# Block sums made in the raw weight buffer, one buffer layout for the whole MLP, and more loads issued by GpSimd, in a one-core hybrid decoder layer

## The chip, the cores and the metric

The kernel runs on one core of a Trainium2 chip. The metric is the device time of one execution in microseconds (us), as a median over runs. The trace belongs to one profiled execution of the same program. In the text TensorE is the engine of matrix products (PE in the profile, with its weight loads shown as PEld), VectorE is DVE, ScalarE is ACT, GpSimd is POOL, and SyncE is SP, which here only issues DMAs. Each engine takes its instructions in the order in which they were put down for it.

## The reference, cut to what matters

One decoder layer with D = 2048, 512 tokens, an MLP width of 8192, all in float32:

```python
mod = silu(c) @ w_ada + b_ada            # six vectors: sh1, sc1, gt1, sh2, sc2, gt2
h = rmsnorm(x) * (1 + sc1) + sh1
q, k, v, xr, xg = split(h @ w_in)        # 3 x 1024 attention, 2 x 1024 recurrence
mixed = concat(rmsnorm(stick_breaking(q, k, v)), rmsnorm(rg_lru(conv(xr)) * gelu(xg)))
x = x + gt1 * (mixed @ w_out)
h = rmsnorm(x) * (1 + sc2) + sh2
hid = square(relu(h @ w_mlp_in))         # 2048 x 8192
x = x + gt2 * (hid @ w_mlp_out)          # 8192 x 2048
return rmsnorm(x, g_norm_final)
```

The change concerns the lines from `mixed @ w_out` to `hid @ w_mlp_out`.

## The kernel before, in words

**Data.** Features lie on the 128 partitions and the 512 tokens in the columns, so a 128x512 tile is one block of 128 features. Every float32 operand of a product is split in two: a high half, which ScalarE makes by a copy into a narrower format, and a low half, which VectorE makes by subtracting the high half from the original (`low`, L115; every low half of the kernel has this line). A product is then three matmuls: high by high, high by low, low by high (`mm3`, and L944 to L946 in the MLP).

**Ordinary products.** `weights` (L193) loads a 128x512 block of weights into `wr` (or `raw` where there is no `wr`), splits it into `wh` and `wl` (ScalarE L207, VectorE L115), and the matmuls of L222 to L226 use it. The output product `mixed @ w_out` is done in four groups of 512 output features. Groups 0 to 2 run on all 512 tokens. Group 3, the last, is done in two token halves A and B of 256 (L872 to L880), so that the norm of half A can begin while half B is multiplied. `out_evac` (L729) then makes x1 = x + gt1 * y, with a scaled addition per tile (L737) and a square and sum for the norm (`add_square`, L299; the sum is L304). Group 0 of `w_mlp_in` is also done by ordinary products in two halves (L885 and L891); at L889 the buffer regions are switched. In all, the last output product and this group are four half products of 16 weight blocks each. The text calls the stretch in which they run the entry to the MLP.

**Block products.** The other 15 groups of `w_mlp_in` and all of `w_mlp_out` use a Strassen-like scheme: a 2x2 arrangement of blocks multiplied by seven products instead of eight. `operands` (L898) loads one block of four quarters (128 x 4 x 256 floats, 512 KB) into `raw` and prepares seven operands: three of the quarters as they are, and four sums of quarters. Per block the instructions are: a sum of 512 columns (L905) and two of 256 (L912, L913), all into a separate tile `ts`; the high copy of three raw quarters by ScalarE (L911, 128x768) and their low half by VectorE (L115, 128x768), both into `w3` tiles; the high copy of the four sums by ScalarE (L917, 128x1024) and their low half by VectorE (L115, 128x1024), both into `w4` tiles. TensorE uses a block in 42 matmuls of 256 columns. `strassen` (L928) runs such blocks, eight to a group in the first phase, into seven PSUM banks, and `combine` (L956) recombines the banks with one ScalarE copy and seven VectorE steps (L960 to L966).

**First MLP phase** (`w_mlp_in`, L1010). After each group `keep_parts` (L827) squares the four results, splits them, forms four sums (L847), and writes all to DRAM as `part` and `sum` through GpSimd's queue. One group is eight blocks.

**Second MLP phase** (`w_mlp_out`, L1084). There are 124 blocks in runs of up to eight for one of four output groups n = 0 to 3. Unfinished banks are written to DRAM as `prod` (GpSimd, L1126) and later loaded back (`load_pre`, L1069, SP) as seed `pre` tiles, which ScalarE copies into PSUM (L934). `load_pair` (L980) brings `part` and `sum` tiles back through SP, and `later_split` splits the sums (ScalarE L994, VectorE L115). Beside it `ada_late` (L1025) makes the last modulation vector: 64 loads of 128x512 into `st` through SP, with one VectorE step each (L1040).

**What sets the order.** The program is written as one sequence; a list scheduler lays it out for each engine by priority. `tc.high_priority` moves a piece forward (URGENT for weights, SETW for `operands`, SETE for evacuations). Side work (norms, `sums`, `keep_parts`, `ada_late`) comes from generators in three lanes, of which `tick` after each weight block takes a few steps. Buffers are pools with a fixed number per name: a new use of a name waits for the old use of the buffer to end. A stage (`STAGES`) is a region of the on-chip memory with its own names; going from one to the next, the new tiles wait for the old ones in that place. Before, there are three: "front", "mlp_in" (`raw` 3, `ts` 2, `w4` 6, `w3` 6) and "mlp_out" (`raw` 3, `ts` 2, `w4` 4, `w3` 4, `pre` 7, `st` 2). `sums` (L806) makes the sums of the activations for the seven products.

The functions that the change touches:

## Time and profile before

| | |
|---|---|
| median of 3 runs | 2160.44 us |
| runs | 2158.01, 2160.44, 2169.7 us |
| profiled execution, whole | 2159.86 us |
| profiled execution, span of the trace | 2158.2 us |
| granted TensorE clock, mean | 0.984 of full speed |
| until 706 us | projections, attention, recurrence, output groups 0 to 2 |
| 706 to 835 us | the entry: last output product, group 0 of `w_mlp_in`, first block products |
| 868 to 1387 us | 13 groups of the first phase |
| 1428 to 1470 us | the turn from the first to the second phase |
| 1512 to 2052 us | most of the second phase |

The profile has a page (busy time of each engine, the span in slices, DMA queues, the chain that ended last, the costliest groups of instructions, DMA issues) and the trace can be asked for parts. In a row of a group of instructions there stand the line, the engine, the operation, output and input tiles, shape and count, then the busy time with the mean of one in ns, then the idle time of the engine just before these instructions with what ended it. `<-ACT w L911` means that the wait ended when ScalarE had written a `w` tile in line 911. All `w3`, `w4` tiles are named `w` there. In rows of a timeline the first number is the start, the second the duration, both in us. In rows of waits, such as `a <- b: 11.0, 2, 10.7`, there stand the time in all, how many, and the longest.

### The profile page before, as it was taken

Reading aid. Unit: us, or ns where it says so; the run is one execution under the profiler, and the core shown is the slowest. Engines: PE = TensorE matmul, PEld = TensorE weight load, DVE = VectorE, ACT = ScalarE, POOL = GpSimd, SP = SyncE. Lnnn points to the kernel's source line nnn. Section 1 sums busy time; section 2 is a strip of 40 time slices with the busy share of each in tenths; the row PEclk is TensorE's granted clock in tenths of the full one; section 3 lists DMA queues with packets and bytes.
Section 4 is the critical chain, followed back from the end, with each engine's and each line's share of the span. In section 5 each row is a group of like instructions: output and inputs, shape, how many; then the busy total and the mean of one; then the engine's idle time right before and its main releaser. Section 6 shows DMA issues by size and latency. Waiting matters only on the chain.

```text
span 2158.2 us, 38620 instructions
## 1 busy us (share of the span) xinstructions
PE 2042.1 (95%) x14532; PEld 1907.9 (88%) x14532; DVE 1800.3 (83%) x3026; ACT 1107.8 (51%) x1657; POOL 180.2 (8%) x276
## 2 busy tenths in 40 slices
...
GB/s 287 281 292 239 202 146 139 164 146 181 234 254 317 252 143 179 165 199 167 150 202 157 167 186 165 191 324 304 259 217 316 304 232 287 254 274 260 309 144 113
DMA packets 225053, 475.06 MB, mean 220 GB/s; under 512 B 22497, under 2 KB 45153, under 8 KB 224866
## 3 DMA queue, kind: packets, MB, share of 16 engines
...
q14 instruction: 73, 0.60, 0.1%
...
## 4 chain that ended last, share of the span: by engine, by line
PE 35%; issue 26%; DMA 16%; DVE 13%; POOL 5%; ACT 3%; SPq 1%; POOLq 0%; DVEq 0%; ACTq 0%
DMA x<-in_w_adaT_dram 5%; PE ps_mm L222 3%; PE ps_mm L226 3%; PE ps_mm L225 3%; DVE w L115 3%; DMA raw<-in_w_mlp_out_dram 3%; POOL part L839 3%; PE ps_mm L946 3%; PE ps_mm L944 2%; PE ps_mm L945 2%; DMA st<-in_w_adaT_dram 2%; POOL sum L848 2%; DMA a<-sum 2%; PE ps_z L946 2%; PE ps_z L944 2%
## 5 line engine op out<-in xcount | busy, mean ns | idle before, releaser
L946 PE MATMUL ps_mm<-a,w 128*128 128x256 f32 x1704 | 483.4, 285 | 10.4 <-DVE w L115 9.9
L944 PE MATMUL ps_mm<-a,w 128*128 128x256 f32 x1704 | 482.9, 284 | 5.5 <-ACT w L911 5.3
L945 PE MATMUL ps_mm<-a,w 128*128 128x256 f32 x1704 | 481.2, 283 | 0.0
L911 ACT ACTIVATE w<-raw 128x768 fp32r<-128x768 f32 x244 | 205.5, 842 | 435.1 <-issue 124.9
L944 PE MATMUL ps_z<-a,w 128*128 128x256 f32 x1288 | 366.1, 284 | 19.9 <-ACT w L911 12.8
L946 PE MATMUL ps_z<-a,w 128*128 128x256 f32 x1288 | 366.5, 285 | 6.2 <-DVE w L115 6.2
L945 PE MATMUL ps_z<-a,w 128*128 128x256 f32 x1288 | 364.3, 283 | 0.0
L946 PEld LDWEIGHTS ps_mm<-a,w 128*128 128x128 f32 x1704 | 322.7, 190 | 15.4 <-DVE w L115 15.0
L944 PEld LDWEIGHTS ps_mm<-a,w 128*128 128x128 f32 x1704 | 324.0, 190 | 7.1 <-ACT w L911 6.1
L945 PEld LDWEIGHTS ps_mm<-a,w 128*128 128x128 f32 x1704 | 323.8, 190 | 0.0
L115 DVE TENSOR_TENSOR w<-raw,w 128x768 fp32r<-128x768 f32 (+1 forms) x262 | 244.5, 934 | 71.0 <-ACT w L911 67.0
L115 DVE TENSOR_TENSOR w<-ts,w 128x1024 fp32r<-128x1024 f32 x244 | 297.6, 1220 | 3.3 <-ACT w L917 3.1
L917 ACT ACTIVATE w<-ts 128x1024 fp32r<-128x1024 f32 x244 | 255.8, 1049 | 42.4 <-DVE ts L913 37.8
L944 PEld LDWEIGHTS ps_z<-a,w 128*128 128x128 f32 x1288 | 244.6, 190 | 22.3 <-ACT w L911 14.0
L946 PEld LDWEIGHTS ps_z<-a,w 128*128 128x128 f32 x1288 | 244.4, 190 | 9.6 <-DVE w L115 9.2
L181 DVE SCALAR_TENSOR_TENSOR x<-x,cb 128x1024 f32<-128x1024 f32 x160 | 195.5, 1227 | 64.0 <-DMA x<-in_w_adaT_dram 63.4
L945 PEld LDWEIGHTS ps_z<-a,w 128*128 128x128 f32 x1288 | 244.7, 190 | 0.0
L207 ACT ACTIVATE wh<-wr 128x512 fp32r<-128x512 f32 x232 | 142.9, 619 | 194.5 <-PE ps_mm L225 90.7
L905 DVE TENSOR_TENSOR ts<-raw 128x512 f32<-128x512 f32 x244 | 167.3, 687 | 69.7 <-DMA raw<-in_w_mlp_out_dram 59.5
L222 PE MATMUL ps_mm<-a,wh 128*128 128x512 f32 (+1 forms) x528 | 201.0, 381 | 8.7 <-DVE a L401 3.1
L226 PE MATMUL ps_mm<-a,wl 128*128 128x512 f32 (+1 forms) x528 | 200.0, 380 | 2.7 <-DVE wl L115 2.6
L115 DVE TENSOR_TENSOR wl<-wr,wh 128x512 fp32r<-128x512 f32 x232 | 158.5, 686 | 50.1 <-ACT wh L207 49.4
...
## 6 DMA issues: line engine op xcount, KB each, us to landing
x<-in_w_adaT_dram SPq DMA_DIRECT2D x160, 512.0 KB, 5.2
raw<-in_w_mlp_out_dram SPq DMA_DIRECT2D x124, 512.0 KB, 4.7
...
wr<-in_w_in_dram SPq DMA_DIRECT2D x160, 256.0 KB, 3.7
...
```

The lines of the kernel that those rows point to most:

```text
L115: tt(out=out, in0=full, in1=f32(high), op=ALU.subtract)
L181: stt(out=t, in0=t, scalar=1.0, in1=cb[q * n // 1024][:, o : o + n], op0=ALU.mult, op1=ALU.mult, accum_out=ga[:, q : q + 1],)
L207: act(h[:, :n], r[:, :n], AF.Copy)
L222: first = mm(out, wh, ah, start=start, stop=False, **kw)
L225: mm(out, wh, al, start=False, stop=False, **kw)
L226: mm(out, wl, ah, start=False, stop=stop, **kw)
L905: tt(out=t[:, : 2 * HT].rearrange("p (a b) -> p a b", a=2), in0=r[:, HT : 3 * HT].rearrange("p (a b) -> p a b", a=2), in1=r[:, q_(0)].unsq ...
L911: act(h, r[:, HT:], AF.Copy)
L917: act(h, t, AF.Copy)
L944: mm(out, wh[:, blk(i)], ah, start=st, stop=False, **kw)
L945: mm(out, wh[:, blk(i)], al, start=False, stop=False, **kw)
L946: mm(out, wl[:, blk(i)], ah, start=False, stop=j == js[-1], **kw)
```

## The change

It has four parts.

1. *Block sums in the raw buffer.* `operands` makes the four sums as four additions of 256 columns in place, in `raw`, one after another (new L924), after the high copy and the low half of the raw quarters have read it. `ts` is gone; the 128x1024 copy and low half now read `raw`. So the old order per block was sums, copy and low half of quarters, copy and low half of sums, and the new order is copy and low half of quarters, sums, copy and low half of sums.
2. *One layout.* The regions "mlp_in" and "mlp_out" become one, "mlp" (`raw` 3, `w4` 6, `w3` 6, `nb` 2), opened ahead of the last output product; the second switch is gone. `n` (5 tiles) becomes permanent. The last output product and group 0 load through `raw` (three buffers, where `wr` had four) and split into `w4`. Seeds use `n` and `nb`, late modulation uses `a`, and the sums of activations two `nb`.
3. *Half products.* A new `half_product` puts four results of 256 columns into two PSUM banks, where four banks were used half. The sums of activations and half operands are made when they are asked for.
4. *Loads and writes by GpSimd.* The 16 writes of x1, the 98 loads of seeds (`pre`) and the 64 loads of late modulation are issued by GpSimd instead of SP.

The core of the diff:

```diff
+BUFS = {"cb": 2, "a": 64, "ga": 4, "n": 5}
 STAGES = {
-    "front": {"x": 3, "tt": 5, "wr": 4, "wh": 3, "wl": 3, "n": 5},
-    "mlp_in": {"raw": 3, "ts": 2, "w4": 6, "w3": 6},
-    "mlp_out": {"raw": 3, "ts": 2, "w4": 4, "w3": 4, "pre": 7, "st": 2},
+    "front": {"x": 3, "tt": 5, "wr": 4, "wh": 3, "wl": 3},
+    "mlp": {"raw": 3, "w4": 6, "w3": 6, "nb": 2},
 }
...
 def operands(src):
             r = T("raw")
             nc.sync.dma_start(r.rearrange("p (c f) -> p c f", c=2), src)
-            t = T("ts")
-            tt(
-                out=t[:, : 2 * HT].rearrange("p (a b) -> p a b", a=2),
-                in0=r[:, HT : 3 * HT].rearrange("p (a b) -> p a b", a=2),
-                in1=r[:, q_(0)].unsqueeze(1).broadcast_to([P, 2, HT]), op=ALU.add,
-            )
             h, lo = T("w3", F32R), T("w3", F32R)
             act(h, r[:, HT:], AF.Copy)
-            tt(out=t[:, q_(2)], in0=t[:, q_(0)], in1=r[:, q_(2)], op=ALU.add)
-            tt(out=t[:, q_(3)], in0=t[:, q_(2)], in1=r[:, q_(3)], op=ALU.add)
             low(lo, r[:, HT:], h)
+            for i, j in ((1, 0), (0, 2), (2, 1), (3, 2)):
+                tt(out=r[:, q_(i)], in0=r[:, q_(i)], in1=r[:, q_(j)], op=ALU.add)
             h, lo = T("w4", F32R), T("w4", F32R)
-            act(h, t, AF.Copy)
-            low(lo, t, h)
+            act(h, r, AF.Copy)
+            low(lo, r, h)
...
+    def half_product(bs, src, operand, ks):
+        for k in ks:
+            wh, wl = weights(src(k), "w4")
+            ah, al = operand(k)
+            for o, out in enumerate(halves(bs)):
+                mm3(
+                    out, wh[:, blk(o)], wl[:, blk(o)], ah, al, k == ks[0] and o % 2 == 0, k == ks[-1],
+                    skip_group_check=True,
+                )
+            tick()
...
+    stage("mlp")
     r2 = T("n")
     order = A_ + L_
-    product(ba, out_src(3), mx, order, A)
+    half_product(b2, out_src(3), mixed_half(A), order)
...
-    for k in range(NK):
-        nc.sync.dma_start(x1D[k], x1[k])
+    for k in range(12, NK):
+        nc.gpsimd.dma_start(x1D[k], x1[k])
...
-    stage("mlp_out")
...
-            t = T("st")
-            tc.keep_in_program_order(nc.sync.dma_start(t, w_adaT[...]))
+            t = T("a")
+            tc.keep_in_program_order(nc.gpsimd.dma_start(t, w_adaT[...]))
...
     def load_pre(n):
-        ts = [T("pre") for _ in range(7)]
+        ts = [T("n" if i < 5 else "nb") for i in range(7)]
         for t, d in zip(ts, prodD[n]):
-            nc.sync.dma_start(t, d)
+            nc.gpsimd.dma_start(t, d)
```

The scheduler lays the instructions out anew. The first place is VectorE at the start of the last output product. The rows are line, operation, output and inputs, shape; `wl` or, after, the second `w4` is the low half of a block of `w_out`; `a` in line 737 (734 after) is an x1 tile of output group 2, and L304 (L301 after) adds its square to the sum for the norm. Before:

```order
L115 TENSOR_TENSOR wl_1345_6573<-wr_1343_6570,wh_1344_6572 128x512
L115 TENSOR_TENSOR wl_1348_6591<-wr_1346_6588,wh_1347_6590 128x512
L737 SCALAR_TENSOR_TENSOR a_1330_6475<-ps_mm_1269_6159,mods_69,n_1331_6476 128x512
L737 SCALAR_TENSOR_TENSOR a_1332_6481<-ps_mm_1270_6160,mods_69,n_1333_6482 128x512
L737 SCALAR_TENSOR_TENSOR a_1334_6487<-ps_mm_1271_6161,mods_69,n_1335_6488 128x512
L115 TENSOR_TENSOR wl_1351_6609<-wr_1349_6606,wh_1350_6608 128x512
L304 TENSOR_TENSOR n_1060_5282<-n_1060_5282,n_1331_6476 128x512
L737 SCALAR_TENSOR_TENSOR a_1336_6493<-ps_mm_1272_6162,mods_69,n_1337_6494 128x512
L115 TENSOR_TENSOR wl_1354_6627<-wr_1352_6624,wh_1353_6626 128x512
```

The same place after:

```order
L734 SCALAR_TENSOR_TENSOR a_1329_6474<-ps_mm_1268_6158,mods_69,n_1330_6475 128x512
L734 SCALAR_TENSOR_TENSOR a_1331_6480<-ps_mm_1269_6159,mods_69,n_1332_6481 128x512
L734 SCALAR_TENSOR_TENSOR a_1333_6486<-ps_mm_1270_6160,mods_69,n_1334_6487 128x512
L301 TENSOR_TENSOR n_1059_5281<-n_1059_5281,n_1330_6475 128x512
L734 SCALAR_TENSOR_TENSOR a_1335_6492<-ps_mm_1271_6161,mods_69,n_1336_6493 128x512
L301 TENSOR_TENSOR n_1059_5281<-n_1059_5281,n_1332_6481 128x512
L301 TENSOR_TENSOR n_1059_5281<-n_1059_5281,n_1334_6487 128x512
L301 TENSOR_TENSOR n_1059_5281<-n_1059_5281,n_1336_6493 128x512
L112 TENSOR_TENSOR w4_1345_6577<-raw_1344_6575,w4_1345_6577 128x512
```

The first low halves of the last output product stood ahead of and between the scaled additions of group 2; now all four scaled additions and all four sums stand ahead of the first low half.

The second place is VectorE in the first MLP phase, blocks near the end of a group, where no recombination step stands between them. The first two rows of a block are the two low halves (of the quarters, 128x768, and of the sums, 128x1024), the others its sums. Before:

```order
L115 TENSOR_TENSOR w3_2265_12530<-raw_2262_12525,w3_2264_12529 128x768
L115 TENSOR_TENSOR w4_2267_12536<-ts_2263_12527,w4_2266_12535 128x1024
L905 TENSOR_TENSOR ts_2286_12660<-raw_2285_12658 128x512
L912 TENSOR_TENSOR ts_2286_12660<-ts_2286_12660,raw_2285_12658 128x256
L913 TENSOR_TENSOR ts_2286_12660<-ts_2286_12660,raw_2285_12658 128x256
L115 TENSOR_TENSOR w3_2271_12588<-raw_2268_12583,w3_2270_12587 128x768
L115 TENSOR_TENSOR w4_2273_12594<-ts_2269_12585,w4_2272_12593 128x1024
L905 TENSOR_TENSOR ts_2296_12732<-raw_2295_12730 128x512
```

After:

```order
L924 TENSOR_TENSOR raw_2379_14484<-raw_2379_14484 128x256 x4
L112 TENSOR_TENSOR w4_2383_14495<-raw_2379_14484,w4_2382_14494 128x1024
L112 TENSOR_TENSOR w3_2386_14545<-raw_2384_14542,w3_2385_14544 128x768
L924 TENSOR_TENSOR raw_2384_14542<-raw_2384_14542 128x256 x4
L112 TENSOR_TENSOR w4_2388_14553<-raw_2384_14542,w4_2387_14552 128x1024
L112 TENSOR_TENSOR w3_2402_14620<-raw_2400_14617,w3_2401_14619 128x768
L924 TENSOR_TENSOR raw_2400_14617<-raw_2400_14617 128x256 x4
L112 TENSOR_TENSOR w4_2404_14628<-raw_2400_14617,w4_2403_14627 128x1024
L112 TENSOR_TENSOR w3_2411_14692<-raw_2409_14689,w3_2410_14691 128x768
```

Before, the sums of a later block (`ts_2286`) stood between the low halves of an earlier one and the next, and a block's sums came two low-half pairs ahead of its own low halves. After, a block is finished from its first low half to its last before the next is begun.

99 lines of the change are left out of this document (51 added, 48 removed).

## The prediction

> **What bounds the kernel now.** I began with the page's first part, to see which engine the span follows.
>
> ```profile
> span 2158.2 us, 38620 instructions
> PE 2042.1 (95%) x14532; PEld 1907.9 (88%) x14532; DVE 1800.3 (83%) x3026; ACT 1107.8 (51%) x1657; POOL 180.2 (8%) x276
> ```
>
> TensorE (PE) is busy 95% and VectorE (DVE) 83%: an average over stages, so I cut the span by stage, with the view of busy time by stretch. The columns are: length, then PE, PEld, DVE, ACT and POOL busy with instruction counts, then granted clock, DMA share, GB/s.
>
> ```profile
> 706.00:823.00 117.00, 97.93 (x772) 94.52 (x771) 96.29 (x198) 78.89 (x160) 0.00 (x0) 0.96 0.62 194
> 786.00:798.00 12.00, 1.36 (x5) 1.07 (x5) 10.39 (x26) 11.72 (x29) 0.00 (x0) 0.69 0.00 0
> 823.00:835.00 12.00, 7.37 (x35) 6.02 (x35) 10.48 (x19) 8.18 (x15) 0.66 (x1) 0.72 0.32 102
> 868.00:1387.00 519.00, 519.00 (x4376) 519.00 (x4375) 470.10 (x704) 267.03 (x364) 89.75 (x130) 1.00 0.55 172
> 1428.00:1470.00 42.00, 27.17 (x175) 25.72 (x174) 37.83 (x63) 21.65 (x33) 12.75 (x20) 0.76 0.81 283
> 1512.00:2052.00 540.00, 515.12 (x4187) 504.87 (x4187) 440.51 (x734) 272.37 (x374) 43.60 (x81) 0.99 0.77 271
> ```
>
> The fourth row is the first MLP phase. There TensorE never stops: 519 us for 4376 matmuls of 256 columns, 0.1186 us each. I use that pace as TensorE's own speed and count matmuls elsewhere. A weight block of the MLP takes 42 matmuls, so 4.98 us.
>
> Entry to the MLP (706 to 835, rows 1 and 3): 807 matmuls, 95.7 us of TensorE, took 129 us, so 33 us are lost. Row 2 is the largest hole: no DMA, half clock. Turn from the first to the second phase (row 5): 175 matmuls are 20.8 us, so 21 of 42 us are lost. Second phase (row 6): 4187 matmuls are 497 us, so 43 of 540 us are lost, at 5.42 us a block. These three stretches, some 97 us, are what the change can win. In row 4 it can only lose. VectorE there is busy 470 of 519 us, so I looked at its spare time next.
>
> ```profile
> L115 DVE TENSOR_TENSOR w<-raw,w 128x768 fp32r<-128x768 f32 x104 | 99.1, 953 | 41.9 <-ACT w L911 41.9
> L917 ACT ACTIVATE w<-ts 128x1024 fp32r<-128x1024 f32 x104 | 108.6, 1044 | 0.1
> L847 DVE TENSOR_TENSOR a<-a,a 128x512 f32<-128x512 f32 x52 | 35.5, 682 | 2.9 <-DMA part<-a 2.1 <-DMA sum<-a 0.6
> L115 DVE TENSOR_TENSOR a<-a,a 128x512 fp32r<-128x512 f32 x39 | 26.6, 683 | 0.0
> 868.65 0.68 DVE L960 TENSOR_TENSOR a<-ps_z,a 128x512 f32<-128x512 f32 x1
> 1386.98 0.68 DVE L960 TENSOR_TENSOR a<-ps_mm,a 128x512 f32<-128x512 f32 x1
> ```
>
> VectorE idles 41.9 us in 519, before the low half of a block's raw quarters (the first subtraction), when ScalarE's copy waits for a buffer that TensorE frees. That is 3.2 us in each of 13 groups of eight blocks. One group takes 39.9 us (the first recombination at 868.65, the one 13 groups later at 1386.98).
>
> **The change part by part.** *Block sums in the raw buffer.* The three additions of a block (one of 512 columns, two of 256) become four of 256, and they overwrite what the first copy and the first subtraction read. So they now stand between the first subtraction and the second copy. VectorE's steps, start to start:
>
> ```profile
> 1007.25 1.22 DVE L115 TENSOR_TENSOR w<-ts,w 128x1024 fp32r<-128x1024 f32 x1
> 1008.38 0.41 DVE L913 TENSOR_TENSOR ts<-ts,raw 128x256 f32<-128x256 f32 x1
> 1008.72 0.68 DVE L905 TENSOR_TENSOR ts<-raw 128x512 f32<-128x512 f32 x1
> 1009.32 0.68 DVE L847 TENSOR_TENSOR a<-a,a 128x512 f32<-128x512 f32 x1
> 1010.86 0.41 DVE L913 TENSOR_TENSOR ts<-ts,raw 128x256 f32<-128x256 f32 x1
> 1011.20 0.95 DVE L115 TENSOR_TENSOR w<-raw,w 128x768 fp32r<-128x768 f32 x1
> 1012.07 1.22 DVE L115 TENSOR_TENSOR w<-ts,w 128x1024 fp32r<-128x1024 f32 x1
> 1014.04 0.42 DVE L912 TENSOR_TENSOR ts<-ts,raw 128x256 f32<-128x256 f32 x1
> 1014.50 0.43 DVE L913 TENSOR_TENSOR ts<-ts,raw 128x256 f32<-128x256 f32 x1
> ```
>
> Independent neighbours take 0.34 (256 columns), 0.60 (512), 0.87 (768) and 1.13 us (1024). A step that needs the one before it starts 0.46 instead of 0.34 us later, so 0.12 more. A block costs VectorE 0.87 + 4 x 0.34 + 1.13 = 3.36 us, after 3.28 before. Eight blocks make 26.9. Fourteen other steps of a group (seven of the recombination, four sums, three low halves; 52 and 39 instructions in 13 groups) add 8.4, and some 17 dependent neighbours 2.0: 37.3 us, which would fit in 39.9.
>
> The wait that this adds decides. The second subtraction needs ScalarE's copy of the finished sums: 1.04 us (the row of 128x1024 above) and two hand-overs, some 1.2. In the new order three of eight blocks have it directly behind the four additions, with nothing between (the rows of VectorE in the section on the change). Queued behind it are the next block's first subtraction and its additions, for which TensorE waits two to three blocks later. So 3.6 us more: 40.9 against 39.9. Thirteen groups make 13 us, less some 5 that the lightly loaded second group wins as a lead. I take **+8**, between 0 (TensorE's pace still rules) and +25 (each of the other five blocks waits 0.25 us too).
>
> By the Trainium skill, "VectorE: DVE Perf Modes", section "The DRAIN you can't avoid", the next operation doesn't start until the pipe is empty, and one should have few of them. That rule speaks against splitting an addition. Here a 256-column step of 0.41 us is followed by the next start after 0.34 us (1010.86 to 1011.20), so I charge start to start.
>
> A raw buffer is held until the second subtraction, and the load that reuses it waits on SP.
>
> ```profile
> SPq L903 <- DVE w L115: 752.8, 209, 6.8
> DMA to landing us min/median/max: 3.5/3.8/5.5
> DMA to landing us min/median/max: 3.6/4.7/9.7
> ```
>
> SP waits there for VectorE today as well. From a second subtraction to the first one of the block three later, the new order has 5.6 to 11 us of VectorE's work. A load needs its landing (3.8 us in the first phase, second row; 4.7 in the second, third row) plus about 1.4 for issue and first copy. So it is free in the first phase and short in about one block of ten in the second.
>
> *One layout, the last output product in it.* No region is switched inside the MLP, so the hole of row 2 goes (the wait of 10.7 below). In its place, all four products of the entry load through three raw buffers; three of them had four `wr`. The last product already runs so:
>
> ```profile
> PE ps_mm L222 <- ACT w L207: 11.0, 2, 10.7
> L222 PE MATMUL ps_mm<-a,w x48: 274/282/581, 796.6 to 822.5; 128*128 128x256 f32 x48
> ```
>
> It runs from 796.6 to 822.5: 26 us for 16 weights, 1.62 a weight, while TensorE alone takes 12 x 0.1186 = 1.42. 64 weights make 104 us. At the start VectorE now finishes the evacuation (one scaled addition and three sums of 0.60) before the first low half: some 3 us. The first MLP block, whose sums come later in its chain and compete with `sums()`, takes about the 12 us of row 3, less 1. So 104 + 3 + 11 = 118 against 129: **-11**. The bounds are -20 (TensorE keeps 1.42) and 0 (1.8 a weight, from a landing of 3.7 us as in the busiest part).
>
> *Two half banks instead of four, sums in `nb`, activation copies of 512.* The matmul and VectorE work is the same: 0. If two banks delayed a product, the evacuation of four 256-column pieces, some 3 us, would show once per product. *Sixteen x1 writes to GpSimd*: it is idle until 823 (0.00 busy in row 1), so 0; on SP they would cost what they cost today.
>
> *Turn between the phases.* VectorE is 37.83 of 42 us busy in row 5, so it is bound there with or without a region switch, and it now has the new waits on top. **-2**, bounds -12 and +8.
>
> *Second phase.* It gets six w4 and six w3 buffers instead of four: a block more of lead. The seed loads (`pre`) and late modulation loads (`st`) leave SP for GpSimd's queue.
>
> ```profile
> L905 DVE TENSOR_TENSOR ts<-raw 128x512 f32<-128x512 f32 x101 | 69.5, 688 | 57.3 <-DMA raw<-in_w_mlp_out_dram 56.0
> L994 ACT ACTIVATE a<-a 128x512 fp32r<-128x512 f32 x46 | 27.1, 622 | 68.4 <-DMA a<-sum 68.2
> L1040 DVE SCALAR_TENSOR_TENSOR st<-st,cb 128x512 f32<-128x512 f32 x57 | 39.0, 685 | 12.7 <-DMA st<-in_w_adaT_dram 12.6
> L1126 POOL DMA_DIRECT2D prod<-a x77 | 41.4, 541 | 434.5 <-ACT a L335 422.3 <-DVE a L337 10.1 <-DMA pre<-prod 1.6
> ```
>
> These are the waits behind the 43 us: 57.3, 68.4 and 12.7 us, 138 in all, in engines that work in order. With VectorE's floor the stretch would take: 26.9 for eight blocks, 7.5 for the rest (57 modulation steps, 48 low halves, 33 copies of 0.60 each and small ones, over 100 blocks), 2.2 of dependence and 4 of ScalarE waits: 40.6, so 5.07 us a block, 506 us for 99.7 blocks instead of 540. The remaining DMA waits are unknown: between 0 (the first phase, where the first additions waited next to nothing) and 138 (all stay, and none is covered). I take 20, nearer to the first phase, because a third set of weights covers a wait of 5 us and the raw loads no longer stand behind seed loads. 526: **-14**, bounds -43 (TensorE's 497) and +104. GpSimd issues 162 more DMAs of 0.54 us in its 434.5 us of idle time; behind a late one stand seed loads that are due 40 us later, so 0. By the Trainium skill, "DMA: Bandwidth & Descriptors", section "SWDGE vs HWDGE vs iDMA", a DMA engine takes its GpSimd and its hardware queues in turn, so a raw load would no longer stand behind a seed load; at the first phase's 3.8 us the sum would be some 10 us lower. No run so far shows it.
>
> Sum: -11 + 8 - 2 - 14 = -19. The profiled execution took 2159.86 us around a span of 2158.2, 0.6 below the median of the three runs (2160.44), so both give **2141**.
>
> **The rivals.** *A, VectorE keeps pace* (its waits fall into time in which TensorE holds the buffers anyway). For it: 41.9 us of such time in 519. Against: the new order puts 3.6 us a group on 3.2. Entry -15, first phase 0, turn -8, second phase -38: **2099**.
>
> *B, slower: VectorE in order with no spare.* ScalarE's split of loaded sums waits for its DMA (68.4 us today); the copy of the block sums stands behind it on ScalarE, VectorE's second subtraction behind that, and three raw buffers stop. Today VectorE makes up such a wait; with 5.07 of 5.42 us used it can't. From 0.35 us of waits a block (35 of the 138 us) the second phase is no longer faster. Half of the 138 gives +35; with +20 in the first phase and -15 elsewhere: **2200**.
>
> *C, no change*: the entry runs at 1.8 us a weight (0), the first phase costs 8, the second wins 8: **2160**.
>
> *D, VectorE pays whole durations*: eight blocks of 0.953 + 4 x 0.419 + 1.22 and 14 of 0.683 make 40.4, with 3.6 of waits 44 a group: +53 in the first phase alone, **2215**. The row pair at 1010.86 speaks against it. It is the skill's rule quoted above, taken at its word.
>
> **How the numbers follow.** Forecast 0.42, A 0.20, B 0.22, C 0.12, D 0.04. The forecast's own range is 2125 to 2158: the entry's and first phase's bounds partly cancel. About 0.5% (11 us) is what a measurement can tell from no change. 0.30 of the forecast lies below 2149.6; with A that is 0.50 faster. 0.12 of it and 0.11 of C are the same: 0.23. B, D and the rest of C make 0.27 slower. The range takes in half of A and most of B: 2095 to 2195.
>
> **What would show it.** Right: the group period in the first phase at 40.5 to 41.5 us, with VectorE waiting for ScalarE's copy of 128x1024; no hole of 10 us before the first phase, and 16 weights in about 26 us in each product of the entry; the second phase near 5.25 us a block. A period of 39.9 would show A; ScalarE waiting for `sum` loads and over 5.4 us a block B. I am wrong if the time changes in the attention part, before 700 us, which should stay as it is.

## The result: slower by 6.8%, and the profile after

The changed kernel takes 2309.78 us (median of 4 runs, 2306.94 to 2312.23), against 2159.61 us of the kernel before beside it (4 runs); the ratio is 1.0684, 95% interval 1.0654 to 1.0713. The forecast was 2141 us in a range of 2095 to 2195. The page's first part after, then the mean granted clock of the core:

```profile
span 2310.5 us, 38553 instructions
PE 2098.2 (91%) x14532; PEld 1948.6 (84%) x14532; DVE 1829.8 (79%) x3270; ACT 1115.9 (48%) x1653; POOL 276.4 (12%) x454
```

```profile
core 0: 2310.5 us, clock 0.963
```

The same 14532 matmuls now fill 91% of a longer span, and VectorE's share fell from 83 to 79%: neither is busier, more time is spent waiting. To see where, I took as marks VectorE's first recombination step of a group (L960 before, L969 after): the first group, the fourteenth, and the first of the last three. First the timeline after with start and duration, then the instructions of the line L969 after and L960 before with, behind the colon, durations (ns) and the first and last start.

```profile
883.14 0.69 DVE L969 TENSOR_TENSOR a<-ps_z,a 128x512 f32<-128x512 f32 x1 [0.50 <-PE ps_z L955]
1443.88 0.69 DVE L969 TENSOR_TENSOR a<-ps_mm,a 128x512 f32<-128x512 f32 x1
```

```profile
L969 DVE TENSOR_TENSOR cb<-ps_mm,cb x1: 683/683/683, 2199.0 to 2199.0; 128x512 f32<-128x512 f32 x1
```

```profile
L960 DVE TENSOR_TENSOR cb<-ps_mm,cb x1: 684/684/684, 2055.9 to 2055.9; 128x512 f32<-128x512 f32 x1
```

| stretch | before, us | after, us | change | forecast |
|---|---|---|---|---|
| to the first recombination (entry) | 868.65 | 883.14 | +14.5 | -11 |
| 13 groups of the first phase | 518.3 (39.87 each) | 560.7 (43.13 each) | +42.4 | +8 |
| turn and second phase, to 2055.9 / 2199.0 | 668.9 | 755.1 | +86.2 | -16 |
| the rest | 102.3 | 111.5 | +9.2 | 0 |

The stretches of the profile after: the last output product and group 0; the 13 groups; twelve groups of the second phase (first to thirteenth set of seeds). Columns as in the prediction.

```profile
716.60:827.00 110.40, 100.11 (x772) 96.51 (x772) 82.88 (x169) 73.05 (x149) 2.16 (x4) 0.97 0.57 176
883.00:1444.00 561.00, 538.04 (x4378) 529.51 (x4378) 481.19 (x809) 275.68 (x366) 88.54 (x130) 0.98 0.51 160
1566.00:2159.00 593.00, 517.91 (x3991) 504.28 (x3990) 430.92 (x801) 264.67 (x368) 118.36 (x219) 0.93 0.65 233
```

**First phase.** TensorE no longer runs through (538 of 561 us), although VectorE's work is what was forecast: 481.19 us in 13 groups is 37.0 a group. VectorE's timeline at the end of a group, merged, with the idle time before a row in brackets, and the waits of this stretch (total, count, longest):

```profile
1172.41 2.09 DVE L112 TENSOR_TENSOR w<-raw,w 128x1024 fp32r<-128x1024 f32 x2 [1.21 <-ACT w L926]
1174.54 1.80 DVE L924 TENSOR_TENSOR raw<-raw 128x256 f32<-128x256 f32 x4
1177.55 2.09 DVE L112 TENSOR_TENSOR w<-raw,w 128x1024 fp32r<-128x1024 f32 x2 [1.21 <-ACT w L926]
```

```profile
DVE w L112 <- ACT w L926: 46.0, 48, 1.2
ACT a L116 <- DMA part<-a: 39.5, 12, 4.3
DVE a L112 <- DMA part<-a: 17.9, 8, 4.3
```

A block goes two subtractions, four additions, a standstill of 1.21 us for ScalarE's copy, and again: 1177.55 - 1172.41 = 5.14 us, over TensorE's 4.98. The standstill makes 46.0 us in 13 groups, 3.5 each (forecast 3.6). A second wait was not forecast: VectorE (17.9 us, 1.4 a group) and ScalarE wait for an `a` tile whose `part` write has not been read out.

**Second phase.** The waits there, then the landing times of raw loads, first after, then before:

```profile
ACT w L920 <- DMA raw<-in_w_mlp_out_dram: 78.8, 18, 8.4
DVE w L112 <- ACT w L926: 56.6, 49, 1.9
DVE w L112 <- ACT w L920: 53.9, 15, 8.7
PE ps_mm L953 <- ACT w L926: 27.5, 10, 6.1
```

```profile
DMA to landing us min/median/max: 3.6/4.7/14.7
```

```profile
DMA to landing us min/median/max: 3.6/4.5/9.7
```

The median landing is nearly the same, the longest is 14.7 instead of 9.7. Of the raw loads of twelve groups whose landing the trace gives, 23 of 78 took over 10 us, before none of 79: a few at each turn of a group are late, ScalarE's first copy waits for them, VectorE for the copy, TensorE for both. VectorE's own work is what was forecast here too (430.92 us for 95 blocks, 36.3 for eight; forecast 26.9 + 7.5 + 2.2 = 36.6), but it idles 162 of 593 us, where the forecast's sum leaves some 70 (526 us less 456 of work for 99.7 blocks). One such turn in TensorE's timeline, and the stretches of 4, 4 and 7 us around it (the granted clock is the third number from the end):

```profile
1877.09 0.28 PE L955 MATMUL ps_z<-a,w 128*128 128x256 f32 x1
1881.50 0.58 PE L953 MATMUL ps_z<-a,w 128*128 128x256 f32 x1 [4.13 <-ACT w L926]
1881.88 0.42 PE L954 MATMUL ps_z<-a,w 128*128 128x256 f32 x1
1883.10 0.58 PE L955 MATMUL ps_z<-a,w 128*128 128x256 f32 x1 [0.80 <-DVE w L112]
1883.48 0.42 PE L953 MATMUL ps_z<-a,w 128*128 128x256 f32 x1
1883.70 0.42 PE L954 MATMUL ps_z<-a,w 128*128 128x256 f32 x1
1883.91 0.41 PE L955 MATMUL ps_z<-a,w 128*128 128x256 f32 x1
```

```profile
1877.00:1881.00 4.00, 0.37 (x4) 0.16 (x2) 4.00 (x12) 1.01 (x2) 0.00 (x0) 0.74 0.00 1
1881.00:1885.00 4.00, 2.70 (x11) 2.40 (x12) 3.97 (x12) 1.18 (x2) 0.00 (x0) 0.50 0.19 66
1885.00:1892.00 7.00, 7.00 (x45) 7.00 (x45) 5.69 (x9) 2.85 (x3) 0.00 (x0) 0.70 0.32 114
```

After a hole of 4.13 us the clock is at half and matmuls start 0.21 us apart (1883.70 to 1883.91), where at full clock it is 0.12 (the 4378 of the first phase took 538.04 us). The clock of 0.70 in the last row is half clock for 4.2 of the 7 us, so from the end of the hole it lasts some 7.7 us and loses up to 3.8: this hole is paid nearly twice. Shorter ones cost less: in the twelve groups TensorE's holes make 593 - 518 = 75 us, and the lost clock (1 - 0.93) x 593 = 42. Over the execution the lost clock is (1 - 0.963) x 2310.5 = 85 us, before (1 - 0.984) x 2158.2 = 35 us. A part of it lies in the holes themselves; TensorE was busy at half clock for 128 us, before for 43, so some 43 of the 152 us come as slower matmuls, not as waits. By the Trainium skill, "TensorE: Matmul & The Clock Gate", section "Part 1: The HAM clock gate", the clock goes to half after an idle window of about 3.4 us and back after a busy one; the trace agrees, with 0.50 behind a hole of 4.13 us, and with half clock in stretches of 3.4 us and multiples of it.

### The profile page after: what moved, and what is told of

Its sections match the earlier page's. It is cut to its first block, busy times and chain, and to the rows that moved or that the text cites. A ratio compares the mean times of both kernels' runs of the same rounds, so it can differ in the third digit from the quotient of the medians.

```text
span 2310.5 us, 38553 instructions
## 1 busy us (share of the span) xinstructions
PE 2098.2 (91%) x14532; PEld 1948.6 (84%) x14532; DVE 1829.8 (79%) x3270; ACT 1115.9 (48%) x1653; POOL 276.4 (12%) x454
## 3 DMA queue, kind: packets, MB, share of 16 engines
q1 hardware_dynamic: 175506, 353.96, 46.7%
## 4 chain that ended last, share of the span: by engine, by line
issue 44%; PE 24%; DMA 12%; DVE 10%; POOL 6%; ACT 2%; SPq 0%; POOLq 0%; DVEq 0%; ACTq 0%
DMA x<-in_w_adaT_dram 4%; PE ps_mm L219 3%; PE ps_mm L223 3%; PE ps_mm L222 3%; POOL part L836 3%; DVE w L112 2%; DMA raw<-in_w_mlp_out_dram 2%; DVE raw L924 2%; DMA n<-prod 2%; POOL sum L845 2%; PE ps_z L223 1%; PE ps_z L222 1%; PE ps_z L219 1%; DVE x L178 1%; PE ps_mm L955 1%
## 5 line engine op out<-in xcount | busy, mean ns | idle before, releaser
L112 DVE TENSOR_TENSOR w<-raw,w 128x768 fp32r<-128x768 f32 (+2 forms) x554 | 565.9, 1040 | 229.9 <-ACT w L926 114.5
L953 PE MATMUL ps_mm<-a,w 128*128 128x256 f32 x1704 | 494.2, 290 | 41.2 <-ACT w L926 38.4
L955 PE MATMUL ps_mm<-a,w 128*128 128x256 f32 x1704 | 493.2, 291 | 27.4 <-DVE w L112 27.1
L954 PE MATMUL ps_mm<-a,w 128*128 128x256 f32 x1704 | 490.4, 288 | 0.0
L926 ACT ACTIVATE w<-raw 128x1024 fp32r<-128x1024 f32 x244 | 257.7, 1057 | 456.5 <-DVE raw L924 411.5
L924 DVE TENSOR_TENSOR raw<-raw 128x256 f32<-128x256 f32 x976 | 400.3, 421 | 14.2
L953 PEld LDWEIGHTS ps_mm<-a,w 128*128 128x128 f32 x1704 | 333.6, 196 | 47.0 <-ACT w L926 42.8
L955 PEld LDWEIGHTS ps_mm<-a,w 128*128 128x128 f32 x1704 | 331.7, 195 | 36.5 <-DVE w L112 36.1
L954 PEld LDWEIGHTS ps_mm<-a,w 128*128 128x128 f32 x1704 | 333.5, 196 | 0.1
L953 PEld LDWEIGHTS ps_z<-a,w 128*128 128x128 f32 x1288 | 250.3, 194 | 43.2 <-ACT w L926 21.7
L955 PEld LDWEIGHTS ps_z<-a,w 128*128 128x128 f32 x1288 | 249.6, 194 | 16.5 <-DVE w L112 16.5
L954 PEld LDWEIGHTS ps_z<-a,w 128*128 128x128 f32 x1288 | 250.7, 195 | 0.0
L204 ACT ACTIVATE wh<-wr 128x512 fp32r<-128x512 f32 (+1 forms) x184 | 113.1, 618 | 172.8 <-PE ps_mm L222 82.0
L223 PE MATMUL ps_mm<-a,wl 128*128 128x512 f32 x448 | 177.8, 398 | 7.6 <-DVE wl L112 7.4
L219 PE MATMUL ps_mm<-a,wh 128*128 128x512 f32 x448 | 178.1, 397 | 5.0 <-DVE a L380 3.4
L222 PE MATMUL ps_mm<-a,wh 128*128 128x512 f32 x448 | 176.8, 395 | 0.0
L112 DVE TENSOR_TENSOR wl<-wr,wh 128x512 fp32r<-128x512 f32 (+1 forms) x184 | 125.9, 686 | 38.6 <-ACT wh L204 38.2
```

The lines of the kernel that those rows point to most:

```text
L112: tt(out=out, in0=full, in1=f32(high), op=ALU.subtract)
L204: act(h[:, :n], r[:, :n], AF.Copy)
L219: first = mm(out, wh, ah, start=start, stop=False, **kw)
L222: mm(out, wh, al, start=False, stop=False, **kw)
L223: mm(out, wl, ah, start=False, stop=stop, **kw)
L924: tt(out=r[:, q_(i)], in0=r[:, q_(i)], in1=r[:, q_(j)], op=ALU.add)
```

## The experiments

All medians with the ratio to the kernel before run beside them. "First" is the mean of 13 groups of the first phase, "second" the mean of 12 groups of the second (from the first to the thirteenth set of seed copies; the expectations go by the median of the steps, up to 2 us lower where one step is long), "entry" the first recombination, all of the profiled execution. The entry is the least exact of them: among the five kernels with separate sums, three `raw` and late modulation on SP, which differ only in when and where the seeds are issued, all of it later, it lies between 870.3 and 883.6.

| kernel | us | ratio, 95% interval | entry | first | second |
|---|---|---|---|---|---|
| before | 2159.61 | | 868.7 | 39.87 | 43.3 |
| after | 2309.78 | 1.0684 (1.0654 to 1.0713) | 883.1 | 43.13 | 49.4 |
| after_loads_on_sp | 2266.55 | 1.0461 (1.0436 to 1.0487) | 886.6 | 43.27 | 45.1 |
| after_separate_sums | 2236.99 | 1.0342 (1.0303 to 1.0380) | 874.6 | 39.92 | 48.0 |
| after_separate_sums_loads_on_sp | 2167.94 | 1.0018 (1.0003 to 1.0033) | 877.3 | 39.88 | 42.4 |
| before_inplace_sums | 2284.68 | 1.0557 (1.0535 to 1.0578) | 864.5 | 43.37 | 47.4 |
| after_loads_on_sp_sums_later | 2307.54 | 1.0669 (1.0651 to 1.0687) | 884.2 | 44.51 | 46.4 |
| after_loads_on_sp_four_raw | 2201.13 | 1.0168 (1.0137 to 1.0198) | 868.0 | 42.38 | 43.1 |
| after_loads_on_sp_sums_later_four_raw | 2263.46 | 1.0462 (1.0425 to 1.0499) | 872.6 | 44.88 | 44.5 |
| after_loads_on_sp_four_raw_half_copies | 2160.90 | 0.9957 (0.9934 to 0.9980) | 873.7 | 40.34 | 41.8 |
| after_four_raw | 2272.68 | 1.0478 (1.0445 to 1.0511) | 861.9 | 42.03 | 48.8 |
| after_separate_sums_seeds_on_gpsimd | 2235.35 | 1.0330 (1.0306 to 1.0354) | 878.4 | 39.90 | 47.4 |
| after_separate_sums_late_mod_on_gpsimd | 2222.29 | 1.0270 (1.0245 to 1.0296) | 878.9 | 40.33 | 45.9 |
| after_separate_sums_seeds_on_scalare | 2193.97 | 1.0112 (1.0083 to 1.0141) | 883.6 | 39.88 | 44.3 |
| after_separate_sums_seeds_on_gpsimd_mid_group | 2217.28 | 1.0244 (1.0197 to 1.0290) | 882.0 | 39.91 | 45.5 |
| after_separate_sums_seeds_on_gpsimd_block_three | 2236.69 | 1.0322 (1.0270 to 1.0375) | 870.3 | 39.94 | 46.7 |
| after_separate_sums_loads_on_sp_four_raw | 2154.84 | 0.9929 (0.9904 to 0.9953) | 869.7 | 39.82 | 42.2 |
| before_late_mod_in_a_five_w4 | 2160.41 | 0.9985 (0.9966 to 1.0003) | 871.3 | 39.87 | 42.7 |
| before_late_mod_in_a_seeds_mid_group | 2177.47 | 1.0060 (1.0036 to 1.0085) | 874.9 | 39.87 | 43.4 |
| before_late_mod_in_a_four_raw | 2163.73 | 1.0000 (0.9973 to 1.0026) | 871.6 | 39.87 | 42.3 |

### Which parts of the change cost: a two-by-two

My theory after reading the trace: two causes, the in-place sums and the loads on GpSimd. The first experiments undo the one, the other, and both, and make the sums alone.

**Loads back on SP**, the seeds (first) and the late modulation's weights.

```diff
-            nc.gpsimd.dma_start(t, d)
+            nc.sync.dma_start(t, d)
...
-            tc.keep_in_program_order(nc.gpsimd.dma_start(t, w_adaT[...]))
+            tc.keep_in_program_order(nc.sync.dma_start(t, w_adaT[...]))
```

> The changed kernel with the seed loads and the late modulation loads issued by SP again; all else as changed. Theory 1 (two causes: the in-place sums slow VectorE in both phases, and the loads on GpSimd come in a bundle at each turn of a group in the second phase and delay the raw loads there): the first phase stays at 43 us a group, the second falls from 49.6 to about 46.5 us a group, 14 turns, so 2310 - 45 = about 2265 us, and no raw load takes over 10 us to land. Theory 2 (the in-place sums alone; the long raw landings only follow from late issue): 2300 to 2315 us and landings over 12 us stay. Theory 3 (the one layout, with three raw buffers and fewer free tiles, is the cause): 2300 to 2315 us as well.

2266.55 us, as theory 1 has it. First phase unchanged, second 45.1; the longest landing of a raw load is back at 9.6 us, here with the stretch of twelve groups:

```profile
DMA to landing us min/median/max: 3.6/4.7/9.6
```

```profile
1575.00:2116.00 541.00, 497.26 (x3994) 484.04 (x3994) 431.67 (x801) 263.80 (x367) 42.95 (x81) 0.99 0.72 256
```

The granted clock of twelve groups is 0.99 again (0.93 after), so the clock lost there came with these turns; over the whole execution it is 0.973, between 0.963 after and 0.984 before.

**Separate sums**, with `operands` as in the kernel before.

```diff
-    "mlp": {"raw": 3, "w4": 6, "w3": 6, "nb": 2},
+    "mlp": {"raw": 3, "ts": 2, "w4": 5, "w3": 4, "nb": 2},
...
+            t = T("ts")
...
-            act(h, r, AF.Copy)
-            low(lo, r, h)
+            act(h, t, AF.Copy)
+            low(lo, t, h)
```

> The changed kernel with the block sums made ahead in a separate ts tile as before (two ts buffers; to make room five w4 and four w3 buffers instead of six and six). GpSimd's loads and the one layout stay. Theory 1: first phase back to 39.9 to 40.5 us a group (some 40 us won), second phase from 49.6 to about 46.5 us (some 45 us won), 2225 us. Theory 2: both phases as before the change, 2150 to 2175 us. Theory 3: no more than 20 us won, 2290 us or more.

2236.99 us, nearest to theory 1: the first phase is fully back (39.92), the second hardly (48.0).

**Both undone**, the two diffs above together.

> Both reverted together: separate sums (two ts, five w4, four w3) and both kinds of loads on SP; what is left of the change is the one layout, the half products, and x1 written by GpSimd. Theory 1: about the time before, 2145 to 2175 us. Theory 2: the same as with separate sums alone. Theory 3: over 2250 us.

2167.94 us: with both undone, the time before is back within 0.3%. The one layout and the half products cost or win next to nothing in sum.

**The in-place sums alone**, in the kernel before with its own buffers.

```diff
-            t = T("ts")
...
+            for i, j in ((1, 0), (0, 2), (2, 1), (3, 2)):
+                tt(out=r[:, q_(i)], in0=r[:, q_(i)], in1=r[:, q_(j)], op=ALU.add)
...
-            act(h, t, AF.Copy)
-            low(lo, t, h)
+            act(h, r, AF.Copy)
+            low(lo, r, h)
```

> The kernel before with only the in-place sums (operands as in the changed kernel); its buffers, regions and queues stay. Theory 1: first phase from 39.9 to 42.5 to 43.2 us a group (13 groups, 35 to 43 us), second phase from 43.4 to about 46.5 us a group (14 groups, 45 us), 2235 to 2255 us. Theory 2: the whole loss, 2290 to 2320 us. Theory 3: 2160 to 2175 us.

2284.68 us, 30 more than theory 1 forecast and 5 less than theory 2; first phase 43.37 (forecast up to 43.2), second 47.4. The in-place sums alone, in the old kernel, make the most of the loss. Its turn and second phase take 736.6 us, 68 more than before; that four w4 and w3 buffers instead of six make this more than in the new layout (+43, below) was not tried by itself.

The turn and second phase (from the fourteenth group's recombination to the first of the last three) as a two-by-two of the changed layout: 662.0 us with neither, 704.8 with the in-place sums (+43), 735.4 with the loads on GpSimd (+73), 755.1 with both (+93). They overlap: 93 is less than 43 + 73. The loads on GpSimd make raw loads land late, with separate sums too (18 of 80 over 10 us); the in-place sums do not (none over 9.6 us with the loads on SP, nor over 9.1 in the old kernel). What those do to a raw load is to hold its buffer longer, so that it is issued later, which the next experiments test. Theories 2 and 3 fall.

### Why the in-place sums cost: VectorE's standstill or the raw buffer

**The sums' subtraction a block later.** `operands` is cut in two, and the second half of a block is put down behind the first half of the next:

```diff
+        held = operands(src(js[0]))
         for j in js:
-            w, a = operands(src(j)), acts(j)
+            now, held = held, operands(src(j + 1)) if j != js[-1] else None
+            w, a = operands_sums(*now, held is not None), acts(j)
```

> The changed kernel with all loads on SP and the sums still in place, but the second subtraction of a block (and its ScalarE copy) put down behind the first subtraction and the four additions of the next block, so that VectorE has 2.7 us of other work while ScalarE copies; the raw buffer is then held a block longer. Theory 1a (the in-place sums cost because VectorE stands still for the copy and for its own last addition): the first phase falls from 43.3 to 40 to 40.7 us a group and the second from 45.4 to 42.5 to 44, so 2266 us becomes 2195 to 2225. Theory 1b (they cost because the raw buffer is held until the second subtraction and the next load comes late): no gain or a loss, 2266 to 2300 us, with ScalarE waiting for raw loads.

2307.54 us, first phase 44.51: theory 1a's number is missed, and theory 1b's 2300 is passed by 8. VectorE no longer waits for the sums' copy, but ScalarE waits for raw loads in the first phase, as theory 1b has it (147.6 us from 884 to 1463; 8.2 in the order before):

```profile
ACT w L920 <- DMA raw<-in_w_mlp_in_dram: 147.6, 49, 4.7
```

Three raw buffers don't allow a block more. That is no verdict on the standstill, so the buffer count was varied by itself.

**Four raw buffers**, for a w4 buffer:

```diff
-    "mlp": {"raw": 3, "w4": 6, "w3": 6, "nb": 2},
+    "mlp": {"raw": 4, "w4": 5, "w3": 6, "nb": 2},
```

> The changed kernel with all loads on SP and four raw buffers instead of three (a w4 buffer is given up for it: five). Sums in place, in the changed order. It is 43.3 us a group in the first phase and 2266 us with three. Theory 1a (VectorE's own standstill behind the additions): no change, 43.0 to 43.4 us a group, 2255 to 2275 us. Theory 1b (the raw buffer held too long): 40 to 41 us a group, 2200 to 2230 us.

2201.13 us: 65 us won, but 18 of them ahead of the first recombination (886.6 to 868.0) and 33 in the turn and second phase (704.8 to 671.4), only 12 in the first phase, which stays at 42.38. So theory 1b is right for the second phase, theory 1a, nearly, for the first (it said 43.0 or more). The 18 us are not the in-place sums': 12 of them lie in the four half products, which load through `raw` but make no block sums (110.5 to 98.6 us), and with separate sums a fourth raw buffer wins as much there (110.8 to 97.9, a kernel shown below); the other 7 lie ahead of the last output product, within the spread of that mark. In the turn and second phase it wins only 5 us with separate sums (662.0 to 657.0), so 28 of the 33 belong to the in-place sums. VectorE's and ScalarE's waits from 900 to 1400 us, with three raw buffers, then with four:

```profile
DVE w L112 <- ACT w L926: 41.0, 43, 1.2
ACT a L116 <- DMA part<-a: 36.2, 11, 4.6
```

```profile
DVE w L112 <- ACT w L926: 46.2, 47, 1.5
ACT a L116 <- DMA part<-a: 7.5, 6, 2.3
```

The standstill stays; the wait for `part` writes, which had not been forecast, goes with the fourth raw buffer (VectorE's own from 22.0 to 5.1 us, 1.4 a group, where the group gains 0.9). Why it does was not tried.

**The later subtraction with four raw buffers**, the two diffs above together.

> The same four raw buffers and five w4, with the second subtraction and its copy put down behind the next block's first subtraction and additions. With three raw buffers this order took 44.5 us a group and 2307 us, with ScalarE waiting 143 us for raw loads in the first phase. Theory 1a: the wait for the copy is gone and the raw loads have their time, 40 to 40.8 us a group, 2195 to 2225 us. Theory 1b alone: as the kernel with four raw buffers in the changed order, or slower. If neither helps, VectorE's work itself is over TensorE's: 42 us a group or more in both.

2263.46 us, 44.88 a group: theory 1a's number is missed. Theory 1b's "or slower" and the third case, over 42 us a group in both, came out, but the next run speaks against VectorE's work as the bound. With the later subtraction the wait moved to ScalarE's first copy, which TensorE's release of a `w3` buffer holds up; the block's second half, put behind it, has lost its lead. The order removed one wait and made another.

**Half copies**, with four raw buffers: ScalarE copies the first two sums while VectorE makes the last two, and VectorE subtracts in two halves.

```diff
-            for i, j in ((1, 0), (0, 2), (2, 1), (3, 2)):
-                tt(out=r[:, q_(i)], in0=r[:, q_(i)], in1=r[:, q_(j)], op=ALU.add)
-            act(h, r, AF.Copy)
-            low(lo, r, h)
+            for half, pairs_ in enumerate((((1, 0), (0, 2)), ((2, 1), (3, 2)))):
+                for i, j in pairs_:
+                    tt(out=r[:, q_(i)], in0=r[:, q_(i)], in1=r[:, q_(j)], op=ALU.add)
+                act(h[:, half * S : (half + 1) * S], r[:, half * S : (half + 1) * S], AF.Copy)
+            for half in range(2):
+                v = slice(half * S, (half + 1) * S)
+                low(lo[:, v], r[:, v], h[:, v])
```

> The changed kernel with all loads on SP, four raw and five w4 buffers, sums in place; ScalarE copies the sums in two halves, the first after two additions, and VectorE subtracts in two halves. VectorE's work grows by about 0.07 us a block, ScalarE's by 0.2. The standstill of 1.2 us behind the additions should shrink to about 0.1 to 0.3 us, while the raw buffer is held as long as before. Theory 1a (that standstill is what is left in the first phase): 42.4 us a group falls to 39.9 to 40.6, and 2201 us to 2150 to 2175. If VectorE's own work is the bound: 42 us a group or more, 2195 us or more.

2160.90 us, first phase 40.34: theory 1a. From 900 to 1400 us TensorE runs without a hole although VectorE has more to do than ever (459 of 500 us), and the standstill is 3.9 us instead of 46.2:

```profile
900.00:1400.00 500.00, 500.00 (x4169) 500.00 (x4168) 459.49 (x867) 273.71 (x443) 82.84 (x122) 1.00 0.53 170
```

```profile
DVE w L112 <- ACT w L927: 3.9, 12, 0.3
```

So in the first phase it was the wait, not the work. With the loads on SP, the buffer and the copy mended, the changed kernel is 0.4% quicker than the kernel before; with separate sums and four raw buffers, below, it is 0.7% quicker.

### Why the loads on GpSimd cost

From here on the kernels have separate sums and all loads on SP, but for what the diff shows. **One kind of load on GpSimd**: first the seeds, then the late modulation's weights.

```diff
-            nc.sync.dma_start(t, d)
+            nc.gpsimd.dma_start(t, d)
```

> Separate sums; the 98 seed loads issued by GpSimd, the 64 late modulation loads by SP. Between both on SP (2168 us, 42.0 us a group) and both on GpSimd (2237, 48.2). If the late modulation loads do it (bundled behind GpSimd's writes of prod at each turn): 2168 to 2185 us here. If the seeds do it (in flight beside the raw loads): 2220 to 2240. If both share: about 2200.

```diff
-            tc.keep_in_program_order(nc.sync.dma_start(t, w_adaT[...]))
+            tc.keep_in_program_order(nc.gpsimd.dma_start(t, w_adaT[...]))
```

> The mirror image: separate sums, the 64 late modulation loads on GpSimd, the 98 seed loads on SP. If the late modulation loads do it: 2215 to 2240 us. If the seeds do it: 2168 to 2185. If both share: about 2200.

2235.35 and 2222.29 us: against 2167.94 either kind alone, with 67 and 54 us, costs most of what both cost (69). "Both share" is wrong too: once one kind is there, the second adds little.

**Four raw buffers in the changed kernel itself**, with its in-place sums and GpSimd's loads; the diff is that of the four raw buffers above.

> The changed kernel as it is (seeds and late modulation on GpSimd, sums in place), with only a fourth raw buffer for a w4 buffer. With the loads on SP the fourth buffer was worth 65 us. If GpSimd's loads cost because they leave too little time for a raw load with three buffers: 2205 to 2225 us, and the second phase near 43.5 us a group. If the cost is separate from the raw buffers: 2245 to 2270 us, 47 to 48 us a group.

2272.68 us, second phase 48.8: the fourth raw buffer, worth 65 us with the loads on SP, is worth 37 here, and only 0.5 us a group in the second phase. Landings up to 14.6 us stay:

```profile
DMA to landing us min/median/max: 3.6/4.8/14.6
```

**The seeds on ScalarE's queue**, a second queue that isn't GpSimd's.

```diff
-            nc.sync.dma_start(t, d)
+            nc.scalar.dma_start(t, d)
```

> Separate sums, late modulation on SP, the 98 seed loads issued by ScalarE's queue instead of GpSimd's (2235 us) or SP's (2168 us). If a second queue beside SP's is what delays the raw loads, whichever it is: 2215 to 2250 us and landings of raw loads over 11 us. If it is GpSimd's queue or its order alone: 2165 to 2185 us and no landing over 10 us.

2193.97 us, between the two: no raw load took over 9.8 us, but the second phase's groups take 44.3 us in the mean instead of 42.4, seven of them as long as on SP (40 to 44), five 45 to 47 (from fourth to fourth seed copy, since here the first copy of a set runs apart from the others). So a second queue as such makes at most 26 of GpSimd's 67 us.

**The seeds on GpSimd, issued later in the group**: a copy of one column on GpSimd waits for the operands of the group's fourth block, and the seeds stand behind it; then of the third.

```diff
+            if before and j == js[min(3, len(js) - 1)]:
+                loaded[0] = before(w)
...
+        gate = nc.gpsimd.tensor_copy(ts[0][:, 0:1], f32(w["11"][0])[:, 0:1])
+        with tc.issue_after(gate.ins):
+            for t, d in zip(ts, prodD[n]):
+                nc.gpsimd.dma_start(t, d)
```

> Separate sums, seeds on GpSimd, late modulation on SP as in the run of 2235 us (47.9 us a group in the second phase), but the seven seed loads are held back until the weights of the fourth block of a group are ready (GpSimd copies one column of them first), so that they are not in flight together with the writes of prod and the pair loads at the turn. If the crowd at the turn is the cause: 41.5 to 43 us a group, 2155 to 2180 us. If GpSimd's queue beside SP's is the cause whenever it is used: 46 us a group or more, 2210 us or more.

2217.28 us: no verdict on the time, since the seeds now came late for ScalarE's seed copies (46.0 us of waits in the twelve groups, none with the seeds at the turn). The raw loads landed sooner: 2 of 78 took over 10 us, with the seeds at the turn 12 of 81.

```diff
-            if before and j == js[min(3, len(js) - 1)]:
+            if before and j == js[min(2, len(js) - 1)]:
```

> Separate sums, seeds on GpSimd, late modulation on SP; the seeds are held back on GpSimd until the weights of the third block of a group are ready, a block earlier than in the run of 2217 us, where ScalarE had to wait for them. With the seeds free at the turn the first raw load issued there lands 18 to 19 us after the first write of prod, with the seeds on SP or ScalarE 15 us. If it is the number of transfers in flight ahead of that load: 14 to 16 us again, 42 to 44 us a group and 2165 to 2195 us. If GpSimd's queue itself slows SP's: 46 us a group or more, 2215 us or more.

2236.69 us: no gain, but no verdict either, since ScalarE waits for late seeds here too, 52.0 us from 1520 to 2080, nearly all in two rows:

```profile
ACT ps_z L949 <- DMA n<-prod: 30.5, 4, 8.4
ACT ps_mm L949 <- DMA n<-prod: 19.8, 3, 9.2
```

The first raw load of a turn was mostly in time, the second stood beside the seeds and landed some 12 us after its issue. So a raw load suffers beside GpSimd's loads away from the turn as well; whether a smaller crowd at the turn would help stays open. How the queues share the DMA engines shows in their packets and bytes: eleven us at a turn of the changed kernel (1863 to 1874), then ten at a turn with separate sums and all loads on SP (1767 to 1777). The columns are packets, MB, share of the engines; q0 is GpSimd's queue, q1 SP's.

```profile
q0 software_dynamic: 815, 2.65, 63.3%
q1 hardware_dynamic: 839, 1.59, 39.3%
```

```profile
q1 hardware_dynamic: 1294, 2.39, 64.1%
q0 software_dynamic: 480, 1.57, 38.8%
```

The engines are full in both (4.24 MB in 11 us are 385 GB/s, 3.96 in ten 396). In the first both queues send packet for packet, 815 to 839; but GpSimd's packets hold 3.25 KB (2.65 MB in 815) and SP's 1.90 KB (in the trace 4096 and 2048 bytes, beside 4-byte ones). Not every stretch is so even: with the seeds alone on GpSimd seven us at a turn show 445 packets to 663. Over the twelve groups after, in the 162 single microseconds in which the engines are full and both queues send, the median ratio is 0.98. So as long as GpSimd has loads, SP's queue, with the raw loads in it, gets 145 GB/s instead of 239 (which then carry the seeds and weights too), and the three raw loads of this turn land in 11.0 to 13.5 us instead of 8.3 to 8.7. With the loads on SP, GpSimd has only the seven writes of prod, and once they are done the engines are SP's. By the Trainium skill, "DMA: Bandwidth & Descriptors", section "SWDGE vs HWDGE vs iDMA", an engine takes its queues in turn and changes at packet boundaries; the counts of the first stretch agree. That this sharing makes the 70 us is inferred from these rows. The seeds on ScalarE's queue fit it: its packets are of 2048 bytes like SP's, no raw load took over 9.8 us, and they cost 26 us instead of 67. But that run changed the queue with the packet size; none changed the packet size alone.

### Versions that might beat both

**Separate sums, all loads on SP, four raw buffers.**

```diff
-    "mlp": {"raw": 3, "ts": 2, "w4": 5, "w3": 4, "nb": 2},
+    "mlp": {"raw": 4, "ts": 2, "w4": 4, "w3": 4, "nb": 2},
```

> A try for a version that beats both: the one layout with separate sums (two ts), all loads on SP, four raw buffers, four w4 and four w3. The fourth raw buffer won 18 us ahead of the first recombination and 33 us in the second phase of the kernel with in-place sums. If it does a part of that here: 2140 to 2160 us. If four w4 and w3 are too few in the first phase (over 40.2 us a group) or the raw buffers were no bound here: 2160 to 2185 us.

2154.84 us, ratio 0.9929 (0.9904 to 0.9953): faster than both, than the kernel before beside it by 0.7%. Four `w4` buffers suffice in the first phase (39.82). Of the 13 us that the fourth raw buffer wins against 2167.94, the half products make nearly all (110.8 to 97.9 us).

**The kernel before with the late modulation's tiles in `a`**, and the room that they leave used for a fifth `w4` buffer, for seeds issued at the sixth block as well, or for a fourth raw buffer in both phases.

```diff
-    "mlp_out": {"raw": 3, "ts": 2, "w4": 4, "w3": 4, "pre": 7, "st": 2},
+    "mlp_out": {"raw": 3, "ts": 2, "w4": 5, "w3": 4, "pre": 7},
...
-            t = T("st")
+            t = T("a")
```

> A try for the best of both: the kernel before, with the late modulation loads (still on SP) into a tiles instead of two st buffers, and the room given to a fifth w4 buffer in the second phase. If these two are what makes the second phase of the changed layout quicker (42.0 us a group with separate sums and SP loads, against 43.3 before): 2140 to 2150 us. If it is the missing region switch: 2155 to 2165.

2160.41 us. The second phase is 0.6 us a group quicker, the rest slower; no difference in sum.

```diff
+            if before and j == js[min(5, len(js) - 1)]:
+                loaded[0] = before(w)
...
-            nc.sync.dma_start(t, d)
+            later(nc.sync.dma_start(t, d))
```

> A try for a version that beats both: the kernel before, late modulation loads into a tiles and five w4 buffers (2160 us, 42.0 us a group in the second phase), and the seed loads put down on SP behind the raw load of the sixth block of a group instead of at its turn. If the crowd at the turn is what keeps the second phase above TensorE's 39.9 us: 40.3 to 41.3 us a group, 2135 to 2150 us. If not: 2155 to 2165 us.

2177.47 us, slower by 0.6%. The steps from first to first seed copy have a median of 41.2 us, but three of them are 58 to 61: only the mark moves there, the first copy of a set running apart from the other six. From fourth to fourth copy every one of the first eleven groups takes 43 to 46 us, with a median of 44.0, against 42.1 with the fifth `w4` buffer alone. ScalarE waits 18.2 us in all for late seeds here, 3.0 at most; whether that makes the difference was not tried.

```diff
-    "mlp_in": {"raw": 3, "ts": 2, "w4": 6, "w3": 6},
-    "mlp_out": {"raw": 3, "ts": 2, "w4": 4, "w3": 4, "pre": 7, "st": 2},
+    "mlp_in": {"raw": 4, "ts": 2, "w4": 5, "w3": 6},
+    "mlp_out": {"raw": 4, "ts": 2, "w4": 4, "w3": 4, "pre": 7},
```

> The kernel before with four raw buffers in both MLP phases (first phase: five w4; second: late modulation in a tiles, four w4). The one layout with four raw buffers and separate sums took 2155 us. If the fourth buffer does the same here: first phase 39.9 us a group, second 41.5 to 42.3, 2145 to 2155 us. If the buffers are no bound here: 2158 to 2168 us.

2163.73 us: no difference. In the old order a raw buffer is released at the first subtraction, and the old entry loads through four `wr`, so three raw buffers suffice.

## Why the prediction was wrong, point by point

- **Sign of the second phase: the step that failed most.** "So it is free in the first phase and short in about one block of ten in the second", 20 us for the remaining waits, and -14 in sum; with the turn -16, measured +86. The work was right (36.3 us for eight blocks, forecast 36.6); the term that failed is the wait, 162 us of VectorE's idle time in twelve groups for some 70. I compared a load's time with VectorE's average work between two uses of a buffer. At the turn shown three raw loads in a row are late, and then ScalarE, VectorE and TensorE wait in a chain. The in-place sums make +43 us of it by themselves, with all loads on SP; 28 of these go with a fourth raw buffer (33, less the 5 that it wins with separate sums). The loads on GpSimd make the rest.
- **Loads on GpSimd: "so 0".** I looked only at who stands behind whom within a queue, and took the two queues' sharing for a gain (10 us by the page of the Trainium skill quoted there). It was 50 us with the in-place sums (704.8 to 755.1) and 73 without. A raw load no longer stands behind seeds, but beside them it gets the smaller part of the bandwidth (1.59 of 4.24 MB in the stretch shown); that this is why is inferred.
- **First phase: mechanism right, size wrong.** The work (37.0 for 37.3) and the standstill (3.5 for 3.6) came out. But 40.9 us was a sum of VectorE's time as if all other waits fell inside; 43.13 has 2 us more. VectorE's wait for `a` tiles, which the sum had at nothing, makes 1.4 of it, and a fourth raw buffer removes 0.9; the rest was not taken apart. The 5 us of lead that I subtracted don't show.
- **Entry: -11, measured +14.5.** The pace was forecast at 1.62 us a weight with bounds 1.42 and 1.8, and came out at 110.4 / 64 = 1.73; with four raw buffers it is 98.6 / 64 = 1.54, so this part of the price was the buffer count. (With 1.42 the sum's own terms give -24, not the -20 of its lower bound.) The hole of 10.7 us did go, but the last output product began 10.7 us later (716.66 for 705.99). The opening of the new region there makes 2.7 of it: between the last matmul ahead of it and the first behind it lie 3 us, start to start, instead of 0.2, in all kernels with the one layout 3 or 4. The 300 matmuls ahead take 77.7 us instead of 72.3, where the kernels with the one layout need 74 to 82 and those with the old ones 72 to 75, so "as it is before 700" was wrong by some 5 us; why is open. The other 2.5 us are earlier and within the spread of the runs. And the first block group took 56.1 us instead of 44.7; with separate sums it is 50.7, with four raw buffers still 55.4. I gave neither the opened region nor this group a price.
- **No term for the clock.** The hole of 4.13 us was followed by some 7.7 us at half clock, and in sum slower matmuls make some 43 of the 152 us. The forecast counted holes once, though row 2 of its own table of stretches showed a clock of 0.69.
- **Rivals.** B, at 2200, named the direction, VectorE without spare and three raw buffers that stop; but its trigger, ScalarE's split of loaded sums, was not the main one: the wait for `sum` loads fell to 24.6 us in the twelve groups after, from 68.4 in the second phase before. A is excluded by 43.13. D's 44 a group is near it, but by luck: the work is 37.0 and not D's 40.4.
